# A transformer trunk layer on one core: zero matmuls ahead of the first loads, and the first stage loaded and ordered by pairs of blocks

## The chip, the core and the metric

The kernel runs on one NeuronCore of a Trainium2 chip. The metric is the device time of one execution in microseconds (us); lower is better. Before the change the median of 3 runs is 931.95 us (930.48 to 932.97).

## The reference

One layer of a trunk with two groups of tokens (128 prompt tokens and 512 latent tokens, 640 in all, width 1024). Each token is modulated by a shift and a scale that come from a conditioning vector, then one input projection feeds three kinds of heads; an output projection, layer norms and a squared-ReLU MLP follow. What matters here is the beginning:

```python
mod = silu(c) @ w_ada + b_ada              # once for c (latent), once for c_ctx (prompt)
sh1, sc1, g1, sh2, sc2, g2 = split(mod, 6) # 1024 columns each
h = x * (1.0 + sc1) + sh1
z = h @ w_in                               # 3328 columns: qa ka va | qb fb_f fb_b ib gb | qc kc vc
g_f = log_forget(fb_f); g_b = log_forget(fb_b)   # group B: a gated scan over chunks of 64 tokens
o_f, s_f = hgrn2_scan(silu(qb), -expm1(g_f), ib, g_f, s0_f)
```

All arithmetic is float32. Products that need its precision are made of three products in the rounded type fp32r: high part by high part, and the two mixed ones of high and low part.

## The kernel before, in words

The width of 1024 is cut into 8 blocks of 128 columns. The first stage runs a loop over these blocks j = 0 to 7 (L239 to L281), and for each it does the following.

- **Loads.** `ada_load` (L198) brings 1024 rows of w_ada, 128 columns of the scale and 128 of the shift, in 4 DMAs of 256 KB, each a set of rows of 512 bytes. `x_load` (L210) brings the block's 128 columns of x: 64 KB of the prompt and 256 KB of the latent tokens. They are issued three blocks ahead on SP's queue.
- **Modulation.** `ada_rows` (L139) multiplies the conditioning `cs` by the block's w_ada on TensorE (L144, fp32) and ScalarE copies the result to `adar` (L146). TensorE transposes x's five tiles (L265, L267) into PSUM `psx` and `psm`, then spreads the modulation rows with `selc` (L270, L271). VectorE makes `sc` and `sh` (L272, L273), ScalarE applies them (L275, L276: `xm`), and `split` (L90) makes the high part `xh` on ScalarE (L91) and the low part `xl` on VectorE (L92). `psx`, `psm` and the PSUM tile of `ada_rows` have one buffer each.
- **The first product.** `first_gemm(j, cols)` (L229) adds block j to three accumulators of 128 columns of w_in each (i = 0, 1: forget gates; i = 2: the query). One third, that is one i, is 6 matmuls (L233 of 384 columns, L234 of 256). It runs two blocks behind the modulation (LAG = 2). Its weights `wfq` come in four loads for two blocks each (`first_load`, called for j = 0, 1, 3, 5 by WPOS), 3 DMAs of 128 KB in rows of 512 bytes, and are split into `wfq_h` and `wfq_l` by ScalarE and VectorE. The raw weights of `wfq` and of the later loads `wib`, `wfb` share two buffers (NWR = 2), so a load waits until VectorE has split the load two before it.

TensorE's order in this stage is the order of the code (`manual_schedule`). The order on the other engines, and on TensorE after this stage, is set by the framework's scheduler; each engine executes its own list strictly in that order, DMA issues on SP's queue as well. After the stage VectorE and ScalarE evacuate the accumulators (L306, L308), TensorE goes on with a product `psib` (weights `wib`), and ScalarE and VectorE turn the first gate into a scan (Exp and Ln at L380 to L392, the scan itself at L393 and L394, then `b_kq` at L486, for which TensorE waits at L489).

```python
                if j >= LAG:
                    first_gemm(j - LAG, (0,))          # L268, between the transposes and the spread
                ...
                if j >= LAG:
                    first_gemm(j - LAG, (1, 2))        # L278, after the split of block j
            for j in range(NK - LAG, NK):
                first_gemm(j, range(3))                # L280
```

Of the kernel before, what the change touches and what calls it, by code (L numbers as in the profile page):

```python
# [11 lines left out]
F32 = mybir.dt.float32  # L12
F32R = mybir.dt.float32r
# [34 lines left out]
MC = 32  # L48
NWS = 5
NWR = 2  # L50
WPOS = (0, 1, 3, 5)

COL_QA, COL_KA, COL_VA = 0, 512, 1024
COL_QB, COL_FF, COL_FB, COL_IB = 1536, 1792, 2048, 2304
# [3 lines left out]
def f32(ap):  # L58
    return ap.bitcast(F32)
# [3 lines left out]
def hybrid_layer_kernel(ctx: ExitStack, tc: tile.TileContext, T):  # L63
# [107 lines left out]
    with ExitStack() as sctx:  # L171
# [7 lines left out]
        nc.scalar.dma_start(ident, T["k_ident"])  # L179
        nc.scalar.dma_start(crow[16:32, :], T["b_ada8"][0:16, :])  # L180
        ps0 = pp.tile([P, 512], F32, tag="misc", name="ps_rows", bufs=NMISC)
        PE.transpose(ps0[:, 0:32], crow, ident[0:32, 0:32])
        b1c = sp.tile([P, 16], F32, tag="b1c", name="b1c")
        V.tensor_copy(b1c, ps0[:, 16:32])
        sil = sp.tile([P, 16], F32, tag="sil", name="sil")
# [9 lines left out]
        V.tensor_tensor(selc, selc, ident[:, 64:66], op=ALU.add)  # L195
        V.tensor_tensor(selc, selc, ident[:, 96:98], op=ALU.add)

        def ada_load(j):  # L198
            parts = []
            for s in range(2):  # L200
                raw = sp.tile([P, 4, 2, P], F32, tag="adar0", name=f"adaw{j}_{s}", bufs=12)
                for i, c0 in enumerate((D + j * P, j * P)):
                    nc.sync.dma_start(
                        raw[:, :, i, :],
                        T["w_ada"][s * 512 : (s + 1) * 512, c0 : c0 + P].rearrange("(k p) n -> p k n", p=P),
                    )
                parts += [raw[:, k].rearrange("p a b -> p (a b)") for k in range(4)]
            return parts

        def x_load(j):  # L210
            x_j = sp.tile([P, NT, P], F32, tag="x", name=f"x{j}", bufs=4)
            csl = slice(j * P, (j + 1) * P)
            nc.sync.dma_start(x_j[:, 0, :], T["x_prompt"][:, csl])
            nc.sync.dma_start(x_j[:, 1:NT, :], T["x_sample"][:, csl].rearrange("(t p) n -> p t n", p=P))
            return x_j

        ahead = 3
        LAG = 2
        ada_q, x_q = [], []
        for j in range(ahead):  # L220
            ada_q.append(ada_load(j))
            x_q.append(x_load(j))
        acc = [pp.tile([P, 512], F32, tag=f"acc{i}", name=f"acc{i}") for i in range(5)]
# [13 lines left out]

        with tc.manual_schedule(engines={mybir.EngineType.PE}):
            for j in range(NK):  # L239
                ada, x_j = ada_q[j], x_q[j]  # L240
                if j in WPOS:
                    first_load(WPOS.index(j))
                if j + ahead < NK:
                    ada_q.append(ada_load(j + ahead))
                    x_q.append(x_load(j + ahead))
                if j == 2:
                    nc.gpsimd.dma_start(rows[0:8, :], T["ln1_g8"])
                    nc.gpsimd.dma_start(rows[8:16, :], T["ln1_b8"])
                    nc.gpsimd.dma_start(rows[16:17, :], T["subln_g"])
                    nc.gpsimd.dma_start(rows[17:21, 0:HD], T["lb_logits_fwd"])  # L250
                    nc.gpsimd.dma_start(rows[17:21, HD:P], T["lb_logits_bwd"])
                    nc.gpsimd.dma_start(rows[21:37, :], T["b_ada8"][24:40, :])
                    mf = sp.tile([P, 4 * CH], F32, tag="mf", name="mf")
                    nc.gpsimd.dma_start(mf, T["k_masks"])
                    G.tensor_copy(masks.rearrange("p a b -> p (a b)"), mf)
                if j == 6:
                    ps1 = pp.tile([P, 512], F32, tag="misc", name="ps_rows1", bufs=NMISC)
                    PE.transpose(ps1[:, 0:37], rows, ident[0:37, 0:37])
                    V.tensor_copy(colc, ps1[:, 0:37])
                    V.tensor_scalar_add(colc[:, 29:37], colc[:, 29:37], 1.0)  # L260
                r = sp.tile([P, 2 * P], F32, tag="adar", name=f"adar{j}", bufs=2)
                ada_rows(r, pp.tile([P, 512], F32, tag="ada", name=f"psada_s{j}", bufs=NADA), ada)
                px = pp.tile([P, 512], F32, tag="xt", name=f"psx{j}", bufs=NXT)
                for t in range(1, NT):
                    PE.transpose(px[:, (t - 1) * P : t * P], x_j[:, t, :], ident)  # L265
                pm = pp.tile([P, 512], F32, tag="misc", name=f"psm{j}", bufs=NMISC)
                PE.transpose(pm[:, 0:P], x_j[:, 0, :], ident)  # L267
                if j >= LAG:  # L268
                    first_gemm(j - LAG, (0,))
                PE.matmul(pm[:, P : P + 2], r[:, 0:P], selc, start=True, stop=True)  # L270
                PE.matmul(pm[:, P + 2 : P + 4], r[:, P : 2 * P], selc, start=True, stop=True)  # L271
                V.tensor_scalar(sc1[:, j, :], pm[:, P : P + 2], b1c[:, 8 + j : 9 + j], 1.0, op0=ALU.add, op1=ALU.add)  # L272
                V.tensor_scalar(sh1[:, j, :], pm[:, P + 2 : P + 4], b1c[:, j : j + 1], None, op0=ALU.add)  # L273
                xm = sp.tile([P, NTOK], F32, tag="xm", name=f"xm{j}", bufs=2)
                A.activation(xm[:, 0:P], pm[:, 0:P], AF.Identity, scale=sc1[:, j, 1:2], bias=sh1[:, j, 1:2])  # L275
                A.activation(xm[:, P:NTOK], px, AF.Identity, scale=sc1[:, j, 0:1], bias=sh1[:, j, 0:1])  # L276
                split(xh[:, j, :], xl[:, j, :], xm)
                if j >= LAG:  # L278
                    first_gemm(j - LAG, (1, 2))
            for j in range(NK - LAG, NK):  # L280
                first_gemm(j, range(3))  # L281


    p1 = big.enter_context(tc.tile_pool(name="p1", bufs=1, reuse_waits="tile"))
# [1600 lines left out]
```

## Time and profile before

| | |
|---|---|
| median of 3 runs | 931.95 us (930.48 to 932.97) |
| the profiled execution's own time | 932.0 us |
| its span, first to last instruction | 930.2 us |
| mean granted TensorE clock | 0.986 |
| busy: TensorE, VectorE, ScalarE | 94%, 71%, 51% of the span |
| chain of waits: TensorE, VectorE, DMA, ScalarE | 70%, 11%, 8%, 6% |
| first 60 us | loads at about 290 GB/s until 47 us; the first product ends at 57.0 us |

A row of the timeline gives the start of a run of like instructions and its length in us, the engine, the line, what is written from what, and in brackets how long the engine stood idle before it and what it waited for. Matmuls overlap, so what one costs in a stream is the distance between starts. A window row gives busy time and count of each engine, then the granted TensorE clock as a share of 2.4 GHz, the busy share of the 16 DMA engines and GB/s.

### The profile page before, as it was taken

The page shows a single profiled execution, that of the slowest core. Times are in us where ns is not written, and L with a number is a line of the kernel's source. Part 1 is how long each engine was busy: PE and PEld are TensorE (multiplying, and loading weights), DVE is VectorE, ACT ScalarE, POOL GpSimd, SP SyncE. Part 2 cuts the span into 40 slices and gives each one's busy share as a digit, 9 for nine tenths or more (in the row PEclk, how much of TensorE's full clock was granted, in tenths as well). Part 3 has the DMA queues.
Part 4 walks back from the last instruction along what each step waited for, and adds up shares of the span by engine and source line. Part 5 has one row for each costly group of instructions (what it writes and reads, how often), then busy time and mean ns, then how long its engine had stood idle before and what let it go on. Part 6 is the DMA issues. An engine that isn't in the chain of part 4 may idle for free.

```text
span 930.2 us, 15406 instructions
## 1 busy us (share of the span) xinstructions
PE 878.0 (94%) x5941; PEld 760.8 (82%) x5941; DVE 663.0 (71%) x1228; ACT 475.9 (51%) x977; POOL 69.0 (7%) x136
## 2 busy tenths in 40 slices
PE   6989898999999998999999899999999999999996
PEld 3888796789889886677788799988998887888885
DVE  2379997988876878895789877676754837663448
ACT  3577666466654647852486545543553606243320
POOL 2200010210101010001000000011000000000000
PEclk9999998999999999999999999999999999999998
DMA  9961524432222202008102544455525835152202
GB/s 260 285 177 50 175 78 138 126 96 58 62 63 63 69 18 91 2 1 294 46 1 70 177 140 148 147 179 183 166 80 200 295 111 176 58 171 88 68 23 91
DMA packets 102314, 109.84 MB, mean 118 GB/s; under 512 B 6720, under 2 KB 82208, under 8 KB 102240
## 3 DMA queue, kind: packets, MB, share of 16 engines
q1 hardware_dynamic: 96256, 92.33, 32.0%
q0 software_dynamic: 5792, 16.44, 5.0%
q8 instruction: 47, 0.77, 0.4%
q14 instruction: 27, 0.22, 0.1%
q10 hardware_dynamic: 192, 0.08, 0.0%
HBM read 96.24 MB, written 12.58 MB: 117 GB/s over the span
## 4 chain that ended last, share of the span: by engine, by line
PE 70%; DVE 11%; DMA 8%; ACT 6%; issue 2%; SPq 1%; DVEq 0%; ACTq 0%
PE psx L1461 10%; PE psy L129 8%; PE psy L131 8%; PE psy L130 8%; PE psz L1461 5%; DMA wad<-in_w_ada 4%; PE psA L130 2%; PE psA L129 2%; PE psA L131 2%; PE psavA L731 2%; PE psy L1461 2%; DMA wf_r<-in_w_ff 2%; PE psavC L953 1%; DVE b_st L561 1%; PE pstA L721 1%
## 5 line engine op out<-in xcount | busy, mean ns | idle before, releaser
L92 DVE TENSOR_TENSOR gl<-hidb,gh 128x640 fp32r<-128x640 f32 x54 | 43.5, 821 | 59.2 <-ACT gh L91 59.2
L1461 PE MATMUL psx<-s,wf3h 128*128 128x320 f32 x256 | 58.6, 315 | 6.6 <-ACT kept L1467 4.5
L91 ACT CAST gh<-hidb 128x640 fp32r<-128x640 f32 x54 | 38.4, 727 | 48.9 <-PE psy L130 40.8
L129 PE MATMUL psA<-wa_h,xh 128*128 128x384 f32 x160 | 54.8, 344 | 0.0
L131 PE MATMUL psA<-wa_h,xl 128*128 128x384 f32 x160 | 54.4, 341 | 0.0
L130 PE MATMUL psA<-wa_l,xh 128*128 128x384 f32 x160 | 54.2, 340 | 0.0
L1467 ACT COPY kept<-psx 128x320 f32<-128x320 f32 x48 | 20.4, 428 | 59.7 <-PE psx L1461 59.7
L1461 PEld LDWEIGHTS psx<-s,wf3h 128*128 128x128 f32 x256 | 43.7, 192 | 7.6 <-ACT kept L1467 4.9
L1347 DVE TENSOR_TENSOR wf3l<-wf_t,wf3h 128x2048 fp32r<-128x2048 f32 (+2 forms) x20 | 37.3, 1864 | 8.2 <-ACT wf3h L1343 8.2
L1461 PE MATMUL psx<-s,wf3l 128*128 128x320 f32 x128 | 40.4, 316 | 0.0
L1343 ACT CAST wf3h<-wf_t 128x2048 fp32r<-128x2048 f32 (+2 forms) x20 | 30.9, 1552 | 5.4 <-DVE wf_t L1320 3.4
L1480 DVE TENSOR_TENSOR st<-psz,kept 128x320 f32<-128x320 f32 x32 | 15.7, 489 | 25.3 <-ACT kept L1467 12.8
L130 PE MATMUL pswo<-wo,mxh 128*128 128x512 f32 x80 | 31.4, 393 | 0.8 <-DVE wo L92 0.8
L129 PE MATMUL pswo<-wo,mxh 128*128 128x512 f32 x80 | 31.5, 396 | 0.5 <-ACT wo L91 0.4
L709 DVE TENSOR_REDUCE nmA<-pssA 128x1 f32<-128x768 f32 x32 | 30.2, 952 | 2.2 <-PE pssA L707 1.9
L129 PEld LDWEIGHTS psA<-wa_h,xh 128*128 128x128 f32 x160 | 30.1, 188 | 2.0 <-issue 1.2
L1527 POOL DMA_DIRECT2D hd<-st x28 | 15.3, 546 | 216.8 <-DVE st L1475 85.0
L131 PE MATMUL pswo<-wo,mxl 128*128 128x512 f32 x80 | 31.2, 390 | 0.0
L711 ACT ACTIVATE pA<-pssA,nmA 128x768 f32<-128x768 f32 x32 | 28.8, 903 | 3.4 <-DVE nmA L709 2.9
L130 PEld LDWEIGHTS psA<-wa_l,xh 128*128 128x128 f32 x160 | 30.2, 189 | 0.2
L131 PEld LDWEIGHTS psA<-wa_h,xl 128*128 128x128 f32 x160 | 30.1, 188 | 0.2
L1461 PE MATMUL psz<-s,wf3h 128*128 128x320 f32 x128 | 29.6, 318 | 0.0
(671 smaller groups left out, 2758.3 us busy)
## 6 DMA issues: line engine op xcount, KB each, us to landing
wad<-in_w_ada SPq DMA_DIRECT2D x32, 512.0 KB, 5.0
wf_r<-in_w_ff SPq DMA_DIRECT2D x32, 512.0 KB, 4.8
hd<-st POOLq DMA_DIRECT2D x28, 320.0 KB, 2.8
hidb<-hd SPq DMA_DIRECT2D x28, 320.0 KB, 4.7
adaw<-in_w_ada SPq DMA_DIRECT2D x32, 256.0 KB, 5.2
wa_r<-in_w_in SPq DMA_DIRECT2D x48, 128.0 KB, 2.7
wo_raw<-in_w_out SPq DMA_DIRECT2D x8, 512.0 KB, 6.5
x<-in_x_sample SPq DMA_DIRECT2D x8, 256.0 KB, 4.8
```

Source lines behind the costliest of these rows:

```text
L91: A.copy(hi, src)
L92: V.tensor_tensor(lo, src, f32(hi), op=ALU.subtract)
L129: PE.matmul(ps, s[0], m[0], start=start, stop=False)
L130: PE.matmul(ps, s[0], m[1], start=False, stop=False)
L131: PE.matmul(ps, s[1], m[0], start=False, stop=stop)
L709: V.tensor_reduce(nm, ps[:, 0:NKEY], axis=AX.X, op=ALU.max, negate=True)
L711: A.activation(pr, ps[:, 0:NKEY], AF.Exp, bias=nm, accum_out=sm[:, col : col + 1])
L731: PE.matmul(po, pT[:, c, :], vals(g, c, c0, n), start=(c == 0), stop=(c == NKC - 1))
L1343: A.copy(h, src)
L1347: V.tensor_tensor(l, src, f32(h), op=ALU.subtract)
L1461: PE.matmul(ps, a_[:, k, :], b_[:, k, :], start=start and k == 0 and i == 0, stop=k == 3 and i == 2, skip_group_check=True)
L1467: A.copy(t, U[u].ps["x"][:, 0:HALF])
```

## The change

Three things in the first stage. (1) VectorE clears a tile `zeros`, and TensorE multiplies it by itself into an accumulator that the first product overwrites later: 12 matmuls of 512 columns before the first transpose, 4 after it, 2 ahead of block 1. (2) Blocks 2 to 7 are loaded in pairs, SPANS (2,2), (4,2), (6,2), so w_ada and x come in rows of 1024 bytes; the weights of the first product for blocks 0 and 1 are loaded ahead of the pair (2,3). (3) TensorE's order goes by pairs (WITHIN, AFTER), and within a third the product by the low weights comes before the one that needs `xl`.

```diff
@@ -179,7 +178,15 @@
-        PE.transpose(ps0[:, 0:32], crow, ident[0:32, 0:32])
+        zeros = sp.tile([P, 512], F32R, tag="zeros", name="zeros")
+        V.memset(f32(zeros), 0.0)
+        acc = [pp.tile([P, 512], F32, tag=f"acc{i}", name=f"acc{i}") for i in range(5)]
+        with tc.manual_schedule(engines={mybir.EngineType.PE}):
+            for _ in range(12):
+                PE.matmul(acc[4], zeros[:, 0:P], zeros, start=True, stop=True)
+            PE.transpose(ps0[:, 0:32], crow, ident[0:32, 0:32])
+            for _ in range(4):
+                PE.matmul(acc[4], zeros[:, 0:P], zeros, start=True, stop=True)
@@ -195,54 +202,71 @@
+        SPANS = ((0, 1), (1, 1), (2, 2), (4, 2), (6, 2))
+        def ada_load(j0, nb):
+            raws = []
             for s in range(2):
-                raw = sp.tile([P, 4, 2, P], F32, tag="adar0", name=f"adaw{j}_{s}", bufs=12)
-                for i, c0 in enumerate((D + j * P, j * P)):
+                raw = sp.tile([P, 4, 2, nb * P], F32, tag=f"adar0{nb}", name=f"adaw{j0}_{s}", bufs=(0, 4, 4)[nb])
+                for i, c0 in enumerate((D + j0 * P, j0 * P)):
                     nc.sync.dma_start(
                         raw[:, :, i, :],
-                        T["w_ada"][s * 512 : (s + 1) * 512, c0 : c0 + P].rearrange("(k p) n -> p k n", p=P),
+                        T["w_ada"][s * 512 : (s + 1) * 512, c0 : c0 + nb * P].rearrange("(k p) n -> p k n", p=P),
                     )
...
+        def x_load(j0, nb):
+            x_j = sp.tile([P, NT, nb * P], F32, tag=f"x{nb}", name=f"x{j0}", bufs=(0, 2, 2)[nb])
...
-        ahead = 3
-        LAG = 2
...
+        for span in SPANS[0:3]:
+            if span[1] > 1:
+                first_load(0)
+            ada_load(*span)
+            x_load(*span)
...
-                for st, mv, first, last in ((h, xh, True, False), (h, xl, False, False), (l, xh, False, True)):
+                for st, mv, first, last in ((h, xh, True, False), (l, xh, False, False), (h, xl, False, True)):
...
+        WITHIN = {2: (1, (1,)), 3: (1, (2,)), 4: (3, (1,)), 5: (3, (2,)), 6: (5, (1,)), 7: (5, (2,))}
+        AFTER = {1: ((0, (0, 1, 2)), (1, (0,))), 3: ((2, (0, 1, 2)), (3, (0,))), 5: ((4, (0, 1, 2)), (5, (0,))),
+                 7: ((6, (0, 1, 2)), (7, (0, 1, 2)))}
...
-                if j in WPOS:
-                    first_load(WPOS.index(j))
-                if j + ahead < NK:
-                    ada_q.append(ada_load(j + ahead))
-                    x_q.append(x_load(j + ahead))
+                if j < 2:
+                    first_load(1 + j)
+                if j in (0, 3):
+                    span = SPANS[3 + j // 3]
+                    ada_load(*span)
+                    x_load(*span)
+                if j == 3:
+                    first_load(3)
...
+                if j == 1:
+                    busy(2)
                 ada_rows(r, pp.tile([P, 512], F32, tag="ada", name=f"psada_s{j}", bufs=NADA), ada)
+                if j in WITHIN:
+                    first_gemm(*WITHIN[j])
...
-                if j >= LAG:
-                    first_gemm(j - LAG, (0,))
...
-                if j >= LAG:
-                    first_gemm(j - LAG, (1, 2))
-            for j in range(NK - LAG, NK):
-                first_gemm(j, range(3))
+            for args in AFTER.get(j, ()):
+                first_gemm(*args)
```

The order changes at three places that matter below. The first is SP's queue, from the load of the first product's first weights (`wfq`). Before:

```order
14 L109 DMA wfq_r_149<-in_w_in 128x2x128 x3
15 L203 DMA adaw_0_161<-in_w_ada 128x4x128 x2
16 L203 DMA adaw_1_164<-in_w_ada 128x4x128 x2
17 L213 DMA x_167<-in_x_prompt 128x128
18 L214 DMA x_167<-in_x_sample 128x4x128
19 L109 DMA wfq_r_197<-in_w_in 128x2x128 x3
```

The change:

```order
10 L108 DMA wfq_r_159<-in_w_in 128x2x128 x3
11 L213 DMA adaw_0_171<-in_w_ada 128x4x256 x2
12 L213 DMA adaw_1_174<-in_w_ada 128x4x256 x2
13 L224 DMA x_177<-in_x_prompt 128x256
14 L225 DMA x_177<-in_x_sample 128x4x256
15 L108 DMA wfq_r_182<-in_w_in 128x2x128 x3
```

The first weights now stand behind two blocks of w_ada and x instead of three, and each w_ada load behind them is twice as wide.

The second place is ScalarE's list at the end of the stage, from the cast of the last `wfq`. Before (`psm_550`, `psx_545` are block 7):

```order
41 L91 CAST wfq_h_430<-wfq_r_428 128x2x2x64 x2
42 L91 CAST wfq_h_430<-wfq_r_428 128x2x128
43 L275 ACTIVATE xm_562<-psm_550,sh_77,sc_76 128x128
44 L276 ACTIVATE xm_562<-psx_545,sh_77,sc_76 128x512
45 L91 CAST wib_h_691<-wib_r_689 128x1024
46 L91 CAST xh<-xm_562 128x640
47 L91 CAST wib_h_697<-wib_r_695 128x1024
48 L380 ACTIVATE b_b_620<-b_b_620 128x640
```

The change (`psm_531`, `psx_526` are block 6, `psm_570`, `psx_559` block 7):

```order
38 L90 CAST wfq_h_348<-wfq_r_346 128x2x128
39 L301 ACTIVATE xm_537<-psm_531,sh_77,sc_76 128x128
40 L302 ACTIVATE xm_537<-psx_526,sh_77,sc_76 128x512
41 L145 COPY adar_542<-psada_s_543 128x256
42 L90 CAST xh<-xm_537 128x640
43 L90 CAST wib_h_687<-wib_r_685 128x1024
44 L301 ACTIVATE xm_570<-psm_564,sh_77,sc_76 128x128
45 L302 ACTIVATE xm_570<-psx_559,sh_77,sc_76 128x512
46 L90 CAST wib_h_693<-wib_r_691 128x1024
47 L90 CAST xh<-xm_570 128x640
48 L389 ACTIVATE lbt<-lbt 128x4
49 L90 CAST wfb_h_950<-wfb_r_948 128x2x2x64 x4
```

The last `wfq` cast now stands ahead of block 6's `xm` instead of block 7's; the second `wib` cast stands ahead of block 7's `xh` instead of behind it; and four casts of the next weights, `wfb`, stand ahead of the accumulators' evacuation.

The third place is VectorE's list there. Before:

```order
42 L272 TENSOR_SCALAR sc_76<-psm_550,b1c 128x2
43 L273 TENSOR_SCALAR sh_77<-psm_550,b1c 128x2
44 L92 TENSOR_TENSOR wib_l_690<-wib_r_689,wib_h_691 128x1024
45 L92 TENSOR_TENSOR xl<-xm_562,xh 128x640
46 L92 TENSOR_TENSOR wib_l_696<-wib_r_695,wib_h_697 128x1024
47 L306 TENSOR_SCALAR b_b_620<-acc_142 128x384
```

The change:

```order
41 L91 TENSOR_TENSOR wfq_l_347<-wfq_r_346,wfq_h_348 128x2x128
42 L298 TENSOR_SCALAR sc_76<-psm_564,b1c 128x2
43 L91 TENSOR_TENSOR xl<-xm_537,xh 128x640
44 L299 TENSOR_SCALAR sh_77<-psm_564,b1c 128x2
45 L91 TENSOR_TENSOR wib_l_686<-wib_r_685,wib_h_687 128x1024
46 L91 TENSOR_TENSOR wib_l_692<-wib_r_691,wib_h_693 128x1024
47 L91 TENSOR_TENSOR xl<-xm_570,xh 128x640
```

Block 6's low part `xl` now comes between block 7's `sc` and `sh`, and block 7's `xl` behind both `wib` splits. After this stage the scheduler's lists of TensorE, ScalarE and VectorE differ in many places for some 1500 of TensorE's matmuls, and are the same from there to the end.

## Rows read from the trace of the kernel before

**Rows 1.** Windows of 3 us in the first stage: busy of PE, PEld, DVE, ACT, POOL, granted clock, DMA share, GB/s.
```profile
20.00:23.00 3.00, 3.00 (x13) 2.62 (x11) 1.10 (x3) 0.94 (x3) 0.00 (x0) 1.00 1.22 290
44.00:47.00 3.00, 3.00 (x25) 2.75 (x27) 0.35 (x2) 1.49 (x3) 0.00 (x0) 1.00 1.16 289
```

**Rows 2.** TensorE's timeline, 5 to 27 us.
```profile
5.42 0.28 PE L182 MATMUL ps_rows<-ident,crow 32*128 32x32 f32 x1 [5.42 <-DMA crow<-in_b_ada]
7.30 1.94 PE L144 MATMUL psada_s<-adaw,cs 128*32 128x256 f32 x16 [1.60 <-DVE cs L193]
9.48 1.11 PE L265 MATMUL psx<-ident,x 128*128 128x128 f32 x4 [0.25 <-DMA x<-in_x_sample]
...
13.21 1.08 PE L144 MATMUL psada_s<-adaw,cs 128*32 128x256 f32 x8 [0.72 <-DMA adaw<-in_w_ada]
...
17.95 1.08 PE L144 MATMUL psada_s<-adaw,cs 128*32 128x256 f32 x8 [0.66 <-DMA adaw<-in_w_ada]
...
20.38 0.69 PE L233 MATMUL acc<-xh,wfq_h 128*128 128x384 f32 x1
...
22.15 0.42 PE L270 MATMUL psm<-selc,adar 128*128 128x2 f32 x2
...
26.33 1.43 PE L144 MATMUL psada_s<-adaw,cs 128*32 128x256 f32 x16
```

**Rows 3.** TensorE's timeline, 31 to 57 us: one whole block from 31.48 to 36.27, then the last eight thirds of the first product, from 49.64 to the start of `psib`.
```profile
31.48 1.07 PE L144 MATMUL psada_s<-adaw,cs 128*32 128x256 f32 x16
32.49 0.66 PE L265 MATMUL psx<-ident,x 128*128 128x128 f32 x4
...
33.01 0.42 PE L233 MATMUL acc<-xh,wfq_h 128*128 128x384 f32 x1
...
33.97 0.28 PE L270 MATMUL psm<-selc,adar 128*128 128x2 f32 x2
...
34.34 0.42 PE L233 MATMUL acc<-xh,wfq_h 128*128 128x384 f32 x1
...
36.27 1.07 PE L144 MATMUL psada_s<-adaw,cs 128*32 128x256 f32 x16
...
49.64 0.42 PE L233 MATMUL acc<-xh,wfq_h 128*128 128x384 f32 x1
...
56.99 0.28 PE L129 MATMUL psib<-wib_h,xh 128*128 128x256 f32 x1
```

**Rows 4.** SP's queue issuing w_ada loads in rows of 1024 bytes later in the kernel, and the window in which only these are transferred (columns as in Rows 1).
```profile
113.03 2.02 SPq L968 DMA_DIRECT2D wad<-in_w_ada  x4
...
115.00:117.00 2.00, 1.52 (x13) 1.50 (x13) 1.96 (x6) 0.76 (x2) 0.00 (x0) 1.00 1.08 378
```

**Rows 5.** ScalarE's timeline at the end of the stage and up to the first scan.
```profile
48.54 1.02 ACT L91 CAST wfq_h<-wfq_r 128x256 fp32r<-128x256 f32 x3 [0.24 <-DMA wfq_r<-in_w_in]
50.43 0.46 ACT L275 ACTIVATE xm<-psm,sh,sc 128x128 f32<-128x128 f32 x1 [0.87 <-DVE sh L273]
50.78 0.77 ACT L276 ACTIVATE xm<-psx,sh,sc 128x512 f32<-128x512 f32 x1
...
52.38 0.73 ACT L91 CAST xh<-xm 128x640 fp32r<-128x640 f32 x1
53.94 1.05 ACT L91 CAST wib_h<-wib_r 128x1024 fp32r<-128x1024 f32 x1 [0.82 <-DMA wib_r<-in_w_in]
57.07 0.74 ACT L380 ACTIVATE b_b<-b_b 128x640 f32<-128x640 f32 x1 [2.09 <-DVE b_b L306]
57.72 0.73 ACT L308 COPY b_q<-acc 128x384 f32<-128x384 f32 x2
...
62.42 0.41 ACT L91 CAST wfb_h<-wfb_r 128x256 fp32r<-128x256 f32 x1 [1.18 <-DMA wfb_r<-in_w_in]
```

**Rows 6.** VectorE's timeline there.
```profile
48.98 1.09 DVE L92 TENSOR_TENSOR wfq_l<-wfq_r,wfq_h 128x256 fp32r<-128x256 f32 x3 [0.76 <-ACT wfq_h L91]
...
52.52 1.23 DVE L92 TENSOR_TENSOR wib_l<-wib_r,wib_h 128x1024 fp32r<-128x1024 f32 x1 [2.19 <-ACT wib_h L91]
53.66 0.82 DVE L92 TENSOR_TENSOR xl<-xm,xh 128x640 fp32r<-128x640 f32 x1
...
64.85 1.48 DVE L393 TENSOR_TENSOR_SCAN b_b<-scanm,b_b 64x640 f32<-64x640 f32 x1
...
70.03 0.42 DVE L92 TENSOR_TENSOR wfb_l<-wfb_r,wfb_h 128x256 fp32r<-128x256 f32 x1
```

**Rows 7.** DMA issues of the two weights that follow: count, KB each, median us from issue to landing.
```profile
wib_r<-in_w_in SPq DMA_DIRECT2D x2, 512.0 KB, 3.8
wfb_r<-in_w_in SPq DMA_DIRECT2D x4, 256.0 KB, 4.9
```

**Rows 8.** TensorE's timeline at two waits for VectorE, a window of 1 us after the first, and one within the second (columns as in Rows 1).
```profile
70.84 0.44 PE L489 MATMUL pskht<-ident,b_kq 128*128 128x128 f32 x2 [3.09 <-DVE b_kq L486]
...
109.83 0.48 PE L500 MATMUL psl<-b_kq,b_k 64*64 64x64 f32 x16 [2.44 <-DVE b_k L529]
...
72.00:73.00 1.00, 1.00 (x10) 0.87 (x10) 0.97 (x6) 1.00 (x4) 0.00 (x0) 0.50 0.00 0
...
109.00:110.00 1.00, 0.17 (x9) 0.20 (x13) 1.00 (x3) 0.00 (x0) 1.00 (x2) 1.00 0.00 0
```

**Rows 9.** POOL's timeline: a memset of 256 float32 columns at the start.
```profile
0.81 0.31 POOL L178 MEMSET cs<- 128x256 f32 x1
```

More of the change, by code (lines that the diff above doesn't have):

```diff
@@ L50 @@
 NWR = 2
-WPOS = (0, 1, 3, 5)
 COL_QA, COL_KA, COL_VA = 0, 512, 1024
@@ L196, in hybrid_layer_kernel @@
         V.tensor_tensor(selc, selc, ident[:, 96:98], op=ALU.add)
-        def ada_load(j):
-            parts = []
+        SPANS = ((0, 1), (1, 1), (2, 2), (4, 2), (6, 2))
+        def ada_load(j0, nb):
+            raws = []
             for s in range(2):
-                raw = sp.tile([P, 4, 2, P], F32, tag="adar0", name=f"adaw{j}_{s}", bufs=12)
-                for i, c0 in enumerate((D + j * P, j * P)):
+                raw = sp.tile([P, 4, 2, nb * P], F32, tag=f"adar0{nb}", name=f"adaw{j0}_{s}", bufs=(0, 4, 4)[nb])
+                for i, c0 in enumerate((D + j0 * P, j0 * P)):
                     nc.sync.dma_start(
                         raw[:, :, i, :],
-                        T["w_ada"][s * 512 : (s + 1) * 512, c0 : c0 + P].rearrange("(k p) n -> p k n", p=P),
+                        T["w_ada"][s * 512 : (s + 1) * 512, c0 : c0 + nb * P].rearrange("(k p) n -> p k n", p=P),
                     )
[L207 to L212, printed above, removed]
+                raws.append(raw)
+            for b in range(nb):
+                ada_q[j0 + b] = [raws[k // 4][:, k % 4, :, b * P : (b + 1) * P] for k in range(NK)]
+        def x_load(j0, nb):
+            x_j = sp.tile([P, NT, nb * P], F32, tag=f"x{nb}", name=f"x{j0}", bufs=(0, 2, 2)[nb])
+            csl = slice(j0 * P, (j0 + nb) * P)
             nc.sync.dma_start(x_j[:, 0, :], T["x_prompt"][:, csl])
             nc.sync.dma_start(x_j[:, 1:NT, :], T["x_sample"][:, csl].rearrange("(t p) n -> p t n", p=P))
-            return x_j
-        ahead = 3
-        LAG = 2
[L219 to L223, printed above, removed]
+            for b in range(nb):
+                x_q[j0 + b] = x_j[:, :, b * P : (b + 1) * P]
+        ada_q, x_q = {}, {}
         w01 = []
@@ L236, in first_gemm, with busy @@
                               skip_group_check=True)
+        def busy(n):
+            for _ in range(n):
+                PE.matmul(acc[4], zeros[:, 0:P], zeros, start=True, stop=True)
+        WITHIN = {2: (1, (1,)), 3: (1, (2,)), 4: (3, (1,)), 5: (3, (2,)), 6: (5, (1,)), 7: (5, (2,))}
+        AFTER = {1: ((0, (0, 1, 2)), (1, (0,))), 3: ((2, (0, 1, 2)), (3, (0,))), 5: ((4, (0, 1, 2)), (5, (0,))),
+                 7: ((6, (0, 1, 2)), (7, (0, 1, 2)))}
         with tc.manual_schedule(engines={mybir.EngineType.PE}):
```

## The prediction

> **What bounds the kernel now.** The change touches only the first 57 us, so I read that stretch first in windows, then along TensorE's timeline, then along the two lists that feed it. The windows show the DMA engines full at 289 to 290 GB/s for rows of 512 bytes, and TensorE full as well from 20 us on [rows 1]. Before that TensorE waits for loads: block 0's x lands at 9.48, the second half of block 1's w_ada at 13.21, of block 2's at 17.95 [rows 2]. It also runs at half clock there: 16 modulation matmuls take 1.94 us at 7.30 and 1.07 at 31.48 [rows 2, 3], the 1.2 and the 2.4 GHz level (the granted clock reads 1.00 in both, so here durations tell it). The higher level comes at about 26.5, within the 16 that take 1.43 [rows 2], after TensorE has worked almost without a pause from 17.95. From there a block takes 4.79 us (31.48 to 36.27): 1.01 modulation, 0.52 transposes, 0.37 spread, the rest three thirds of the product [rows 3]. Eight thirds run from 49.64 to 56.99, 0.91 each. The product thus starts at 20.38 [rows 2] and ends at 56.99, some ten us after the loads.
>
> **The loads.** A block is 1.05 MB of w_ada and 0.33 MB of x, a `wfq` load 0.39 MB. Block 2's w_ada is complete at 3.80 MB and 17.95 us, the last `wfq` at 12.58 MB and 48.54 [rows 2, 5]: 8.78 MB in 30.6 us, 287 GB/s. Nothing here shows w_ada of the first stage in rows of 1024 bytes; the nearest row is w_ada later, with nothing beside it: 378 GB/s [rows 4]. The ends are 290 (the row size is worth nothing) and 378; I take 378, since it is the same tensor, queue and row size. The Trainium skill's page "DMA: Bandwidth & Descriptors" (Specifications) speaks against it: line rate needs 512 bytes or more, so pairs would bring nothing. By that rule the stage would stay at 290; by the rows, 512 bytes are not enough, and the first rival is what becomes of the time if the rule holds.
>
> With 378 for blocks 2 to 7 and 290 for the rest, landings become: first `wfq` 15.7; pair (2,3) w_ada 21.3, x 23.0; `wfq` 24.3; pair (4,5) 29.9 and 31.6; `wfq` 33.0; pair (6,7) 38.5 and 40.2; last `wfq` 41.6 instead of 48.5. Pair (6,7) reuses the buffers of (2,3), so SP waits for block 3's modulation, done at 24.9 below; data is queued until 33, so it costs nothing until that step is some 3 us later than that.
>
> **The zeros.** VectorE's memset has 512 columns where POOL's 256 took 0.31 [rows 9]; about 0.6, done by 1.5. The first zero matmuls go at half clock: a step of 384 and 256 columns is 0.295 (six such in 20.38 to 22.15 [rows 2]), so 512 columns are about 0.43 each, 12 of them 5.1. The transpose at 5.42 then comes up to 1.2 late and block 0's modulation may start at 8.5. Even at 1.94 us it ends at 10.4, one us after x landed; block 1's w_ada comes at 13.2, so this is hidden, and so are the 4 and the 2 other zeros (1.7 and 0.9 at most). If the higher level is reached there, does it hold through waits under 2 us? A wait of 2.44 at 109.83 left the granted clock at 1.00, one of 3.09 at 70.84 was followed by 0.50 [rows 8]; I take it as held.
>
> **TensorE by pairs, at full clock.** Block 0's product can start at 16.2; four thirds (block 0, and one of block 1) end near 20.0. Pair (2,3) waits for w_ada to 21.3, for x to 23.0. Then the lists matter. `xm` and `xh` take 1.1 and 0.7 us on ScalarE [rows 5], `xl` 0.82 on VectorE [rows 6]; with one PSUM buffer block 3's transposes wait for block 2's `xm`, which stands behind the `wfq` cast (24.3 + 1.0): 26.4. `xl` of a pair's first block stands behind the second block's `sc`, so TensorE stalls half a us in the first third after each pair. Pair (2,3) ends at 31.5. From there nothing waits for loads: two blocks cost 2 x (1.01 + 0.52 + 0.37) + 6 x 0.91 = 9.3, with stalls of 0.5 and 0.1 some 9.8. So (4,5) ends at 41.3, and (6,7) reaches its last three thirds at 50.3.
>
> There they wait. The last `wfq` split (1.09, [rows 6]) ends at 45.9 on VectorE and frees the buffer of the second `wib`, which takes 3.8 to land [rows 7]: 49.8. Its cast (1.05, [rows 5]) now stands ahead of block 7's `xh`, which is ready at 51.5, and both `wib` splits (1.23) ahead of `xl`, ready at 52.8: 1.2 and 0.7 of waiting. The product ends at **54.9 instead of 57.0, 2.1 earlier**: the gain of a start four us earlier and at full clock, less what the new order gives back.
>
> **Past the stage.** What counts is the first scan, at 64.85 [rows 6]. Before, ScalarE's first Exp starts at 57.07 and the scan 7.8 later; 1.18 of this is ScalarE waiting for `wfb` at 62.42 [rows 5]. After, `wfb` is issued when VectorE has split the first `wib` (49.6) and lands 4.9 later [rows 7], 54.5; four casts (0.33 each) and the evacuation (0.7) precede the Exp: 56.5. From there the wait of 1.18, the evacuation (0.7) and one cast are gone, another Exp of 0.65 is ahead: 6.2, the scan at 62.7. Also 2.1 earlier, so both ways into the next stretch move alike, and TensorE's wait of 3.09 for `b_kq` stays. Of the `wfb` splits three more fall before the scan, where VectorE has time; each occupies it 0.42 [rows 6], so up to 1.2 is taken from a stretch in which VectorE hardly rests. TensorE is full in parts of it, so I count half, 0.6. The reordered lists after that can win or lose as the waits fall; I take zero, and 3 us (one wait like those of 2.44 and 3.09) either way for the range.
>
> **Sum.** 932.0 (the profiled execution's own time, 0.05 from the median of 931.95) - 2.1 - 0.6 = **929.3**; this case's own range is 927.5 to 931.
>
> **The rivals.**
> - *The pairs come no faster* (chance 0.13). At 290 GB/s pair (4,5) has its w_ada at 33.8, its x at 36.0 and the `wfq` ahead of `xm` at 37.4; the point that decides is x, which TensorE needs at 33.4. The pair ends at 44.6 instead of 41.3. For (6,7) x lands at 46.9 and the last `wfq` at 48.2: its casts end at 49.2, `xh` of block 7 comes at 55.7, `xl` at 57.0, the product ends at 59.1, 2.1 later than before: 934.1. For it: the windows of this stage are flat at 290 [rows 1]. Against it: 378 [rows 4].
> - *The zeros do not do what they are there for* (0.15): TensorE is back at half clock when the product starts. 24 matmuls at 0.295 instead of 0.15 cost 3.5, less the 1.3 it would have waited for w_ada: 2.2. All that follows moves along: the product ends at 57.1, the scan is where it was, and only the splits' 0.6 is left: 931.4. For it: with waits of 0.25 to 1.60 between its work from 5.42 to 17.95 TensorE stayed at the lower level [rows 2], and such waits are still there.
> - *The gain is given back by the next weights* (0.12): if `wfb` lands 2 us later than taken, four casts ahead of the evacuation hold the Exp to 58.5 and the scan to 64.7. Only the splits' 0.6 is left: 931.3. For it: these casts stand there now; against it: less traffic then.
> - *The stalls are shorter than replayed* (0.15): the replay has 3.6 us of them in the three pairs. Half gone is 927.5, all gone with the whole 1.2 of the splits 925.1.
>
> **How the numbers follow.** The forecast has 0.45. 0.3% is 2.8 us, about what a measurement of this kernel can tell from no change: the line is at 929.15, close to the forecast, which gives 0.25 to faster, 0.18 to the same, 0.02 to slower. Shorter stalls give 0.15 to faster. Half clock gives 0.01, 0.12, 0.02; late weights 0.01, 0.09, 0.02; slow pairs 0, 0.05, 0.08, where a reordered wait decides. Together 0.42, 0.44, 0.14. The range goes from all stalls gone, 925.0, to the slow pairs, 934.2.
>
> **What would show it.** In the profile after: matmuls of zeros from about 1.5 us; 16 modulation matmuls of block 0 or 1 in 1.07; about 370 GB/s between 16 and 40 us where rows of 1024 bytes move; the last `wfq` cast near 43 instead of 48.54; the first product from 16 to about 55; waits of about half a us at each pair's `xl` and about 2 us at block 7's `xh` and `xl`; the first scan near 62.7. I am wrong if the windows stay at 290, if the modulation of block 1 still takes twice its time, if the product ends before 53 or after 57, or if the difference at 65 us is not the difference at the end.

## The result, and the profile after

The changed kernel takes 941.02 us (median of 5 runs, 938.2 to 942.48), the kernel before 932.97 beside it (5 runs): ratio 1.0078, 95% interval 1.0059 to 1.0098 (here and below a ratio is to executions of the kernel before taken beside the run). It is **slower by 8 us**, outside the forecast's range. The first part of its profile, to be read against the table of before: the span is 939.2 us.

```profile
span 939.2 us, 15400 instructions
PE 885.9 (94%) x5959; PEld 766.0 (82%) x5959; DVE 662.7 (71%) x1229; ACT 474.6 (51%) x977; POOL 69.0 (7%) x136
```

The start first. TensorE's timeline of the changed kernel, as [rows 2, 3]:

```profile
1.46 5.04 PE L186 MATMUL acc<-zeros 128*128 128x512 f32 x12 [1.46 <-DVE zeros L182]
...
8.28 1.07 PE L143 MATMUL psada_s<-adaw,cs 128*32 128x256 f32 x16 [0.47 <-issue]
...
21.48 0.64 PE L143 MATMUL psada_s<-adaw,cs 128*32 128x256 f32 x8 [1.41 <-DMA adaw<-in_w_ada]
...
23.98 0.63 PE L293 MATMUL psx<-ident,x 128*128 128x128 f32 x4 [0.78 <-DMA x<-in_x_sample]
...
32.55 1.07 PE L143 MATMUL psada_s<-adaw,cs 128*32 128x256 f32 x16
...
43.24 1.07 PE L143 MATMUL psada_s<-adaw,cs 128*32 128x256 f32 x16
...
50.29 0.44 PE L245 MATMUL acc<-xl,wfq_h 128*128 128x384 f32 x1 [0.35 <-DVE xl L91]
...
53.29 0.45 PE L245 MATMUL acc<-xh,wfq_h 128*128 128x384 f32 x1 [0.68 <-ACT xh L90]
...
54.66 0.44 PE L245 MATMUL acc<-xl,wfq_h 128*128 128x384 f32 x1 [0.51 <-DVE xl L91]
...
56.82 0.28 PE L128 MATMUL psib<-wib_h,xh 128*128 128x256 f32 x1
```

Block 0's modulation is at full speed (1.07 us for 16). The pairs start at 21.48, 32.55 and 43.24, `psib` at 56.82, 0.2 us earlier than before. The loads, in a window (columns as in [rows 1]; the last is GB/s), and then ScalarE and VectorE up to the scan, as [rows 5, 6]:

```profile
15.00:40.00 25.00, 21.88 (x181) 17.38 (x181) 7.86 (x23) 11.56 (x26) 0.69 (x1) 1.00 1.10 342
```

```profile
56.25 1.33 ACT L90 CAST wfb_h<-wfb_r 128x256 fp32r<-128x256 f32 x4 [1.19 <-DMA wfb_r<-in_w_in]
...
58.11 1.37 ACT L404 ACTIVATE b_b<-b_b 128x640 f32<-128x640 f32 x2
```

```profile
64.15 1.48 DVE L417 TENSOR_TENSOR_SCAN b_b<-scanm,b_b 64x640 f32<-64x640 f32 x1
```

The scan stands at 64.15, 0.70 earlier than before [rows 6]. So in this execution the change is ahead at 65 us, and the loss comes later. One execution is not enough for that, though. Eight profiles have the new start and the changed kernel's lists up to there (this one, e5, e7, e9, e12, e13, e14 and e18 below): their scans stand between 64.13 and 65.85, 64.9 in the mean, no earlier than the 64.85 of before. With the old lists (e1, e6, e8, e10, e11, e17) they stand between 63.40 and 64.28, 63.8 in the mean. So the lists cost about 1 us ahead of the scan already.

TensorE's waits behind the stage, as [rows 8]:

```profile
70.13 0.44 PE L513 MATMUL pskht<-ident,b_kq 128*128 128x128 f32 x2 [2.15 <-DVE b_kq L510]
...
82.69 0.41 PE L128 MATMUL psfb<-xh,wfb_h 128*128 128x320 f32 x1 [1.50 <-ACT mixed L450]
...
145.50 0.77 PE L1001 MATMUL psada<-selc,ada 128*128 128x2 f32 x4 [2.49 <-ACT ada L145]
...
205.21 0.49 PE L803 MATMUL pscs<-cqkA 64*128 64x128 f32 x4 [2.03 <-ACT cqkA L723]
```

The last of these in the kernel before:

```profile
195.50 0.49 PE L779 MATMUL pscs<-cqkA 64*128 64x128 f32 x4 [0.90 <-ACT cqkA L699]
```

The windows of the changed kernel:

```profile
85.00:90.00 5.00, 5.00 (x30) 4.88 (x25) 4.12 (x10) 1.79 (x4) 0.00 (x0) 0.50 0.35 105
...
170.00:175.00 5.00, 4.78 (x37) 4.20 (x38) 2.03 (x10) 1.56 (x5) 0.00 (x0) 0.81 0.68 211
175.00:180.00 5.00, 5.00 (x44) 4.49 (x43) 1.36 (x4) 0.79 (x3) 0.00 (x0) 0.85 0.01 3
```

A reader should see three things: the wait of 1.50 at 82.69, followed by the lower clock level (0.50); VectorE busy for only 3.4 of the 10 us from 170 to 180 while TensorE is full; and `pscs`, the first product that needs the last head's result, at 205.21, where the kernel before has it at 195.50.

**A balance.** From the first `psib` matmul to the ninth `pscs` matmul (269.43 before, 279.54 after) every kernel without fillers does the same TensorE work. I add up windows of 1 us: idle is 1 less PE's busy share, lost clock is 1 less the granted clock. What is left is the work, and without fillers it comes out alike within 2 us:

| one profiled execution of | length | idle | lost clock | rest |
|---|---|---|---|---|
| before | 212.4 | 14.2 | 5.1 | 193.1 |
| changed | 222.7 | 16.2 | 13.7 | 192.9 |
| e1 new start, old lists | 213.2 | 13.0 | 8.5 | 191.7 |
| e2 old start, new lists | 224.8 | 21.0 | 10.2 | 193.6 |
| e11 new start, old lists, filled | 207.4 | 6.6 | 0.0 | 200.9 (fillers in it) |

In these two profiles the 10.3 us between before and after are idle time (+2.0) and half clock (+8.5). A spell of half clock costs 1.7 us or about twice that here, and how many there are changes from one execution to the next: the mean granted clock of the kernel before lies between 0.978 and 0.991 in 112 executions. So a single profile is good to some 2 to 4 us at best, and e1's is of its slowest execution (935.56), e10's of its quickest (933.01); the verdicts below go by medians.

The granted clock of every execution is on record, and it corrects the balance. The span times (1 less the granted clock) is, in the mean, 15.2 us for the kernel before and 18.2 for e2 beside it; 16.1 for e1 and 18.6 for the changed kernel. So with the new lists come some 3 us of half clock, not 8.5. As TensorE's work is the same, the larger part of the 10 us must be time in which TensorE waits.

### The profile page after: what moved, and what is told of

It reads as the page before. It is cut to its first block, busy times and chain, and to the rows that moved or that the text cites. A ratio compares the mean times of both kernels' runs of the same rounds, so it can differ in the third digit from the quotient of the medians.

```text
span 939.2 us, 15400 instructions
## 1 busy us (share of the span) xinstructions
PE 885.9 (94%) x5959; PEld 766.0 (82%) x5959; DVE 662.7 (71%) x1229; ACT 474.6 (51%) x977; POOL 69.0 (7%) x136
## 4 chain that ended last, share of the span: by engine, by line
PE 66%; DVE 12%; DMA 9%; ACT 8%; issue 3%; SPq 1%; POOL 0%; DVEq 0%; ACTq 0%; POOLq 0%
PE psx L1485 10%; PE psy L128 7%; PE psy L129 7%; PE psy L130 7%; PE psz L1485 5%; DMA wad<-in_w_ada 3%; PE psA L128 2%; PE psavA L755 2%; PE psA L130 2%; PE psA L129 2%; DMA wf_r<-in_w_ff 2%; PE psy L1485 2%; PE psavC L977 1%; DVE b_st L585 1%; PE pstC L745 1%
```

## Experiments

The change alters the scheduler's lists behind the stage (57 to 225 us), though no line there is edited: 130 new neighbours on TensorE's list, 200 on VectorE's, 139 on ScalarE's, 15 on SP's. To part the start from the lists, a list can be imposed: each instruction is chained to its predecessor on its engine by an order-only edge.

```python
def keep_order(tc, nc):                  # called behind hybrid_layer_kernel(tc, aps)
    by = {i.name: i for i in nc.cur_bb.bb.instructions}
    for eng, text in ORDER.items():      # per engine, the other kernel's order as instruction numbers
        ...
            tc.add_manual_dep(i, prev.name, NoSync, reason="order")
```

**e1: new start, old lists.** 

> The changed kernel's first stage whole, but on every engine's list the instructions behind the first product stand in the order of the kernel before (each chained to its predecessor by an order-only edge). Theory 1 (the loss lies in the rearranged lists behind the stage): the 0.7 us that the trace shows gained at the first scan stays to the end, 932.3 us (931.3 to 933.3), TensorE's half-clock loss from 57 to 215 us back at about 5 us. Theory 2 (the loss comes from the new start itself: its loads, buffers and later weights delay what follows): about 941 us as in the changed kernel.

931.04 us, ratio 0.998 (0.9962 to 0.9999), just under the range of theory 1; the half-clock loss in its profile is 8.5 us and not 5. First scan 63.85, and the lead of 0.7 to 1.0 us is still there at the scan at 110.89 (before 111.63).

**e2: old start, new lists.** 

> The mirror image: the first stage of the kernel before, and behind the first product every engine's list in the changed kernel's order. Theory 1 (the lists): 941.7 us, the changed kernel's time and the 0.7 us of the start lost again (940.5 to 943), half-clock loss of about 13.7 us from 57 to 225 us. Theory 2 (the start): 933 us as before.

943.40 us, ratio 1.0119 (1.0093 to 1.0145), just over the range of theory 1. The crossing is clean: by the medians the new start is worth -2.4 us with either lists (barely clear of nothing in e1's interval), the new lists are worth +10 with either start. Theory 2 is out.

**e3: the zeros left out.**
```diff
-                PE.matmul(acc[4], zeros[:, 0:P], zeros, start=True, stop=True)   # 12, 4 and 2 of them
```


> As the first run here, without the zeros (the memset of the zero tile, 12, 4 and 2 matmuls). If the loads set the end of the first stage, it makes no difference: within 0.3 us of the first run, first product's last columns at 55 to 57 us still. If TensorE's own work sets it, blocks 0 and 1 run at half the clock (16 modulation matmuls in 2.1 us and not in 1.07) and the end comes 1 to 2 us later: 933.5 to 934.5 us.

931.92 us, ratio 0.9984 (0.9964 to 1.0005); not told apart from e1. TensorE's timeline without zeros:

```profile
7.29 1.93 PE L143 MATMUL psada_s<-adaw,cs 128*32 128x256 f32 x16 [1.60 <-DVE cs L194]
...
13.45 1.08 PE L143 MATMUL psada_s<-adaw,cs 128*32 128x256 f32 x8 [0.62 <-DMA adaw<-in_w_ada]
...
23.06 1.07 PE L143 MATMUL psada_s<-adaw,cs 128*32 128x256 f32 x16
```

Half speed up to 14 us and longer, full from 23.06 on, and the scan only 0.3 later than e1's (64.17): the zeros work, but in e1 what they speed up then waits 1.41 and 1.04 us for loads (at 21.80 and 24.55), and here these waits are gone.

**e4: one harmless line.**
```diff
-((h, xh, True, False), (h, xl, False, False), (l, xh, False, True))
+((h, xh, True, False), (l, xh, False, False), (h, xl, False, True))
```


> The kernel before with one line of the change: the three products of each weight tile of the first product in the order high x high, low x high, high x low. Same work, loads and waits in the stage, so the scan at 65 us moves by less than 0.5 us; but the lists behind it come out rearranged (126 new neighbours on TensorE's list, 182 on VectorE's). Theory 1: the time moves by some us either way, over 0.3% from before, with the difference arising after 70 us. Theory 2 (start alone): within 0.3% of before, 930.5 to 935.

938.60 us, ratio 1.0064 (1.0041 to 1.0087), with the first scan at 64.97 (64.85 before). An edit that leaves the first scan within 0.1 us in these profiles costs 5 us. That it costs them through the lists is argued from e1 and e2; the swap with the old lists held was not run.

**e5, e6, e17, e18: which stretch of the lists.** Cut at about 85 us:
```diff
 TensorE 0-249, VectorE 0-73, ScalarE 0-67, SP 0-11
-as in the one kernel
+as in the other
```


> The changed kernel's start; the lists of the changed kernel up to about 85 us (TensorE's 250th instruction behind the stage, VectorE's 74th, ScalarE's 68th, SP's 12th), from there those of the kernel before. Theory 1a (each rearranged stretch costs its own part): the 2.4 us by which the changed kernel's second scan at 92 us stands behind that of the first experiment, no more: 933.4 us (932 to 935). Theory 1b (the first rearranged stretch sets off everything behind it): 940 to 941 us.

> The changed kernel's start; the lists of the kernel before up to the same cut at about 85 us, from there those of the changed kernel. Theory 1a: the changed kernel without the 2.4 us of the first stretch, 938.6 us (937 to 940). Theory 1b: as in the first experiment, 931 to 932 us.

934.64 (ratio 1.002, 1.0001 to 1.004) and 941.01 us (1.0083, 1.0058 to 1.0107): new lists cost 3.6 us ahead of the cut and 10.0 behind it, against e1. Cut at about 158 us: 

> The changed kernel's start; the lists of the kernel before up to about 158 us (TensorE's 735th instruction behind the stage, VectorE's 245th, ScalarE's 183rd, SP's 27th), from there those of the changed kernel. If the loss sits behind 158 us (the chain of the last head: psu, recurrence, psl, psu, recurrence, pscs): 938 to 941 us. If it is spread over the lists: half of the 10 us, 935 to 937 us. If it sits ahead of the cut: 931 to 932 us.

> The reverse: the changed kernel's lists up to the same cut, from there those of the kernel before. If the loss sits behind 158 us: 932 to 935 us, the 3 us of the first stretch and no more. If it is spread: 935 to 937 us. If it sits ahead of the cut: 939 to 941 us.

937.60 (1.0054, 1.0035 to 1.0074) and 937.08 us (1.0043, 1.0028 to 1.0059): 6.6 behind, 6.0 ahead. The loss is spread; theory 1b is out, and the parts add up to somewhat more than the whole (12.6 and 13.6 against 10).

**e7, e8, e11, e16: is it the clock?** Matmuls whose result is overwritten, in TensorE's waits:
```diff
+    def fill(ps, n):
+        for _ in range(n):
+            PE.matmul(ps, xh[:, 0, 0:P], xh[:, 0, 0 : ps.shape[1]], start=True, stop=True)
...
+            if (h, p0) == (0, 0): fill(pt, 9)              # all four runs, in the pskht tile itself
+            if (h, p0) == (1, 2): fill(pt, 10)             # all four runs
+            if (h, p0) == (2, 2): fill(pt, 10)             # e11, e16: in a later pskht, a tile of its own
...
+                if (h, p0) == (0, 2): fill(ps2[:, 0:512], 6)   # e7 alone
...
+        if c0 == 4864: fill(pm[:, 256:512], 20)            # e7, e8: in the tile that ScalarE copies
```


> The changed kernel with its own lists, and TensorE kept busy in four of its waits by matmuls whose result is overwritten: 9 of 512 columns at 70 us, 6 of 512 at 82 us, 10 of 512 at 111 us, 20 of 256 at 145 us, each group some 0.2 to 0.4 us shorter than its wait. The waits stay, only the clock can change. Theory A (most of the loss is half clock behind the waits): the spells at 70 to 75, 84 to 92, 111 to 116 and 145 to 153 us go, 10.2 us of lost clock, and the time is 931 to 936 us. Theory B (the waits themselves are the loss and the clock spells stand beside other limits): 940 to 942 us.

> The first experiment (the changed kernel's start, the order of the kernel before behind it) with three of its waits filled in the same way: 9 matmuls of 512 columns at 70 us, 10 of 512 at 109 us, 20 of 256 at 143 us. Theory A: the spells at 70 to 75 and 142 to 150 us go, 5.1 us of lost clock, 926 us (925 to 928), faster than both kernels. Theory B: 931 us as in the first experiment, or up to 1 us more where a filler outlasts its wait.

943.17 us (1.0107, 1.0082 to 1.0132) and 931.88 us (0.9986, 0.9971 to 1.0001). Neither theory was tested cleanly, as e8's row shows:

```profile
141.86 3.87 PE L311 MATMUL psada<-xh 128*128 128x256 f32 x20 [2.56 <-ACT ada L145]
```

The 20 fillers write columns of the tile that ScalarE is copying, so they wait 2.56 us like the matmul they were to cover, and then take 3.87 more, most of it at the lower level (e7's wait 2.48 and take 4.16). Still, e7's executions have no more half clock than those of the kernel before beside them (15.2 us in the mean in both) and take 10 us longer, of which the late fillers can be some 4. With another tile: 

> As the eighth run, but the fillers at 143 us go to another tile (10 of 512 columns into pskht22, a bank that nobody reads then), since in the eighth run they queued behind the very copy that the wait is for and ran 3.9 us behind it. Theory A (half clock behind the waits costs its full 1.7 us a spell): spells at 70 and 142 gone, 926 to 927.5 us. Theory B (the waits' own length is what counts): 930.5 to 931.5 us.

928.89 us, ratio 0.9959 (0.9939 to 0.9979): **faster than both kernels**. The windows of e11 and then of e1 at the first and third wait (columns as in [rows 1]):

```profile
69.00:73.00 4.00, 3.02 (x32) 2.62 (x32) 3.88 (x16) 3.42 (x12) 0.00 (x0) 1.00 0.00 0
...
142.00:147.00 5.00, 5.00 (x94) 3.23 (x93) 4.73 (x16) 3.89 (x12) 0.00 (x0) 1.00 0.77 211
```

```profile
69.00:73.00 4.00, 3.17 (x22) 2.91 (x23) 3.88 (x16) 3.44 (x12) 0.00 (x0) 0.74 0.00 0
...
142.00:147.00 5.00, 4.36 (x62) 3.28 (x66) 3.87 (x14) 3.60 (x13) 0.00 (x0) 0.56 0.57 159
```

No lost clock at all from 57 to 225 us in e11, against 5.1 us before and 8.5 in e1. In medians it gained 2.2 us on e1 (2.0 by the ratios), between the two theories and less than the 3.5 to 5 that the first expected. Over all executions e11 has 10.1 us of half clock and e1 16.1, so a us of half clock taken away gave back about 0.4 us of time (an estimate from these two runs). And without the new start: 

> The kernel before, start and order, with the three waits at 70, 110 and 143 us filled as in the eleventh run (9, 10 and 10 matmuls of 512 columns). If the filled waits carry the eleventh run's gain: 5.1 us of lost clock back, 928 to 930.5 us. If they help only with the new start: 932 to 934 us.

931.08 us, ratio 0.9978 (0.9963 to 0.9994), between the two expectations and nearer the first. The fillers are worth 0.2% on either start, the new start 0.2%, and e11 is the sum.

**e9, e10, e12, e13, e14: is it one place?** The changed kernel's trace has a suspect at 170 to 180 us. TensorE, then ScalarE, then VectorE:

```profile
171.92 0.66 PE L578 MATMUL psu<-mixed,b_kht 64*128 64x64 f32 x8
...
178.47 0.43 PE L578 MATMUL psu<-mixed,b_kht 64*128 64x64 f32 x2
```

```profile
178.94 0.20 ACT L587 COPY b_st<-psu 64x64 f32<-64x64 f32 x1 [4.79 <-PE psu L578]
```

```profile
178.57 0.42 DVE L642 TENSOR_TENSOR zA<-psA,rope_c 128x256 f32<-128x256 f32 x1 [5.01 <-PE psA L130]
```

The last of ten `psu2` matmuls (the trace counts each twice) is listed behind the 24 of `psA02`, and two engines idle 5 us until the recurrence `b_st` can start.

```diff
 TensorE's list: psu2 (nine)
+psu2 (the tenth)
 psA02 (24)
-psu2 (the tenth)
 pskht30
```


> The changed kernel with its own lists but for one matmul: the tenth of the ten matmuls of tile psu2, which stands behind the 24 of tile psA02 (172.5 to 178.5 us), is moved ahead of them, behind the ninth. Theory C (the loss of the second stretch is this one place: ScalarE's copy and VectorE's state recurrence wait for the tenth matmul, 4.8 and 5.0 us idle, and everything of that head is late): the recurrence starts at 172 to 174 us and not at 179.4, the product pscs at 199 to 200 and not at 205.2, the time is 935 us (934 to 937). Rival D (the time is bounded by TensorE's total work and its clock, this wait stands beside it): 939 to 942 us.

> The reverse: the first experiment (the changed kernel's start, the order of the kernel before) with the tenth matmul of psu2 moved behind the 24 of psA02. Theory C: VectorE and ScalarE idle some 4 to 5 us before 178 us, 936 us (934 to 938). Rival D: 931 to 932 us as in the first experiment.

e10: 937.76 us (1.0048, 1.003 to 1.0067), **6.7 us for one matmul placed late** (against e1 by the medians, 6.3 by the ratios). Its TensorE and VectorE, and then e1's TensorE:

```profile
175.58 0.72 PE L524 MATMUL psl<-b_kq,b_k 64*64 64x64 f32 x16 [4.38 <-DVE b_stn L585]
```

```profile
169.80 4.34 DVE L585 SCALAR_TENSOR_TENSOR b_st<-b_st,b_dec,psu 64x64 f32<-64x64 f32 x14 [4.95 <-ACT b_st L588]
```

```profile
175.23 0.48 PE L524 MATMUL psl<-b_kq,b_k 64*64 64x64 f32 x16 [0.19 <-DVE b_stn L585]
```

This profile of e10 is of its quickest execution, so it shows the price in this place alone: from the first `psu` matmuls of this head (162.57, in e1 166.91) to `psl` it is 13.0 us, in e1 8.3.

e9, the repair: 943.36 us (1.0092, 1.0063 to 1.012), **nothing gained**; theory C as put fails. Its VectorE shows a reason: three `zA02` instructions that need all of `psA02` stand ahead of the recurrence there.

```profile
176.03 0.43 DVE L642 TENSOR_TENSOR zA<-psA,rope_c 128x256 f32<-128x256 f32 x1 [3.66 <-PE psA L130]
...
176.71 0.26 DVE L585 SCALAR_TENSOR_TENSOR b_st<-b_st,b_dec,psu 64x64 f32<-64x64 f32 x1
```

```diff
 ScalarE's list: b_kq (6 ACTIVATE)
+mixed<-psib (the last copy)
 b_d (4), b_kq, b_kht, b_k
-mixed<-psib (the last copy)
```


> The ninth run with a second place mended: ScalarE's copy of the last psib tile, which TensorE's first psfb matmul waits for at 82.7 us (1.50 us, and half clock from 84 to 92 us behind it), is moved ahead of seven other ScalarE instructions of that list. If these two places are the whole loss: 931.5 us (930 to 933), the time of the first experiment. If the first place gives nothing that lasts: the ninth run's time, 935 us.

945.07 us (1.0119, 1.0096 to 1.0142). Neither expectation was met. The wait at 82 us moved on to `pslv`, which waits for VectorE's `b_lqk`, and the lower clock level (84 to 91 us) stayed:

```profile
81.24 0.39 PE L128 MATMUL psfb<-xh,wfb_h 128*128 128x320 f32 x1
...
83.40 0.57 PE L524 MATMUL pslv<-b_lqk 128*64 128x64 f32 x12 [1.77 <-DVE b_lqk L540]
```

```diff
 VectorE's list: b_k, b_d, a, b
-zA02 (three)
 b_st0 (14), b_stn2
+zA02 (three)
```


> The changed kernel's own lists with the tenth psu2 matmul ahead of psA02 as in the ninth run, and on VectorE's list the three zA02 instructions, which wait for psA02, moved behind the recurrence on b_st0, where the kernel before has them. Theory C' (this place, on both lists, is the loss of the second stretch): the recurrence starts near 173 us and not at 176.7, pscs at 198 to 200 us, the time is 935 us (933 to 938). Theory D (the loss is spread over the lists, another wait takes over): 940 to 943 us.

942.56 us (1.0103, 1.0079 to 1.0127). The recurrence does start early now, at 172.07, but `psl` behind it stands after 17 `psA` matmuls on TensorE's list, and VectorE waits for that instead:

```profile
172.07 4.34 DVE L585 SCALAR_TENSOR_TENSOR b_st<-b_st,b_dec,psu 64x64 f32<-64x64 f32 x14 [0.93 <-ACT b_st L588]
...
182.16 0.30 DVE L564 COPY_PREDICATED b_att<-masks,psl 128x128 f32<-128x128 uint8 x1 [3.14 <-PE psl L524]
```

```diff
 TensorE's list
-psfb30 (1) pslv02 (24) psl802 (12) psada3072 (2) psfb30 (23)
+psfb30 (6) pslv02 (24) psada3072 (2) psfb30 (8) psl802 (12) psfb30 (10)
```


> As the run before, and the first stretch mended on both lists too: TensorE's list between the first and the last psfb30 matmul in the order of the kernel before (six psfb30 matmuls and more stand between the others again), ScalarE's copy of the last psib tile ahead of seven instructions. If the two places are the whole loss: 931 to 933 us, the first experiment's time. If the loss is spread: 938 us or more.

939.59 us, the median of five executions (1.0092, 1.0066 to 1.0119); a sixth took 2152.6 us and is left out; there is no profile of it, and its cause stays open. The wait at 84 us is down to 1.04, but `pscs` still waits 3.24 and comes at 203.48. So these two places are not the loss.

**e15: the loads of the start.**
```diff
             for s in range(2):
+                if (j0, s) == (2, 1):
+                    raws.append(raws[0])
+                    continue
```


> The first experiment with half of w_ada of blocks 2 and 3 not loaded (the first half's rows are used twice, so their modulation is another): 1.05 MB less ahead of x of blocks 2 and 3, at the 340 GB/s of that stretch 3.1 us. If the loads before 24 us set the start, the waits of 1.4 and 1.0 us at 21.8 and 24.6 us go and the first scan comes 2.4 us earlier, at 61.4 us, the time is 928.6 us (927.5 to 930). If TensorE's own work sets it: the scan stays at 63.8, the time at 931.

928.94 us (0.9962, 0.9944 to 0.9979): 2.1 below e1 by the medians, by the ratios 1.7, and the two intervals overlap. The waits at 21.8 and 24.6 are gone, but in the profiled execution the scan is at 64.07 and `psib` at 57.60 (e1 57.58). There the clock was at its lower level in the start, zeros or not, so this profile does not tell what the loads set at full clock:

```profile
15.00:20.00 5.00, 4.97 (x20) 4.57 (x20) 2.17 (x6) 2.87 (x6) 0.74 (x1) 0.50 1.09 336
```

## Why the prediction was wrong, point by point

- **The zeros**: right in place and effect (1.46 us; 16 modulation matmuls in 1.07). "I take it as held" was right in the profiled execution, not in each: of the 15 profiles with zeros seven have the lower level from 15 to 20 us (e15's row, and e9, e10, e12, e13, e14, e17). It hardly matters: e10 is one of them and has the earliest scan of all, 63.40, and without the zeros the scan is 0.3 later and the time does not change measurably (e3), where the rival took 2.2 us for it. In the working, 0.295 us is the mean of matmuls of 384 and 256 columns, by which 512 columns take 0.47 and not 0.43; the trace has 0.42.
- **The loads**: 378 GB/s taken, 342 measured from 15 to 40 us. x of the second pair came at 23.98, not 23.0. That the DMAs of this part set the start is hinted at by e15's time and not shown. The Trainium skill's page "DMA: Bandwidth & Descriptors" (Specifications) gives 512 bytes as enough for line rate; the traces differ: 290 in rows of 512 bytes [rows 1], 342 where most are of 1024.
- **TensorE by pairs**: from 32.55 to 43.06 (where the next pair's work begins) took 10.5, not 9.8, and the product ended near 56.8, not 54.9. Gain 0.2 of 2.1, and in the other 14 profiles with zeros none: there `psib` starts between 56.99 and 58.63 (56.99 before). So this term failed too, in its size.
- **Past the stage**: the `wib` loads took 5.3 us to land (median of two), not 3.8, `wfb` landed at 56.25, not 54.5, and four casts held the first Exp to 58.11 (56.5 forecast). That is the rival "given back by the next weights", nearly to its price: it put the scan at 64.7, it came at 64.15. In e1, whose ScalarE list has the Exp ahead of those casts, it is at 63.85. With the lists held, 931.04 us is then 1.7 from the forecast, but by luck in part: in e1 the product ends 0.6 later than before and the Exp starts at 57.36 (57.07 before). What brings the scan forward stands behind the Exp (6.5 us to the scan instead of 7.8): ScalarE's wait of 1.18 for `wfb` is gone, as forecast.
- **The splits**: five `wfb` splits before the scan instead of two, as said; what they give could not be seen beside the rest.
- **The failed step** is "The reordered lists after that can win or lose as the waits fall; I take zero, and 3 us ... either way for the range". The lists cost 10 us (e1 against the changed kernel, e2 against before). No rival priced them either, since all of them changed a wait within the stage or just behind it. The last sentence of the forecast, that it is wrong "if the difference at 65 us is not the difference at the end", is what happened: -0.7 at the scan in the profiled execution, +8 at the end.
- **What of the lists costs it**: shown is that the loss is spread over at least two stretches (e5, e6, e17, e18), that one matmul placed late can cost 6.7 us (e10), and that mending one or two places hands the wait to another instruction and gains nothing measurable (e9, e12, e13, e14). A chain through three engines (`psu`, copy, recurrence, `psl`, `b_kq`, and again) is slowed wherever one link stands behind independent work, on any of the three lists (shown at this one place, argued for the rest). Half clock is the smaller part: some 3 us more of it come with the new lists (18.2 us in e2, 15.2 before), and e11 and e1 together say that taking a us of it away gives back about 0.4. Which waits make up the remainder of the 10 us stays open.

## What to carry to other kernels

Where a scheduler orders the lists, an edit is two changes: what it does, and the new lists it sets off. Compare the lists first, hold them with order-only edges to time the edit by itself, and put the lists' own price (here 10 us of 930 for this change, and 5 us for a swap that changes no work) into the range. A profile is one execution: set several beside each other before a us is believed. A wait that cannot be removed can be filled with matmuls (0.2% here), but only into a tile that nobody is reading.

## What the runs showed of the hardware

- TensorE's clock dropped to its lower level behind waits that left it there 1.5 us idle (82.69 in the changed kernel, then 0.50), and from 15 to 20 us in seven of the 15 profiles with zeros (0.50 to 0.66 in e9, e10, e12 to e15 and e17; 1.00 in the changed kernel and e1) although TensorE was busy alike in both, 4.8 to 5.0 of these 5 us and 3.0 to 3.1 of the 5 before; behind the filled waits of e11 and e16 it never did from 57 to 225 us.
- The granted clock reads 1.00 at the start of e3 (6 to 15 us), while matmuls took twice their later time (8 in 1.08 us, later 16 in 1.07): the row of a matmul tells that level, the column does not.
